# DoRA forward: W split into 125 and 3 partitions, block 0 loaded in four parts, and the last three chunks of block 4 loaded as single chunks with the first stores due one chunk earlier

## The chip, the core and the metric

The kernel runs on one core of a Trainium2 chip. The metric is the time of one execution on the device in microseconds (us). The version before the change has a median of 164.68 us over 14 runs (162.11 to 165.88).

## The reference

x has 16 x 2048 rows of 256 numbers (fp32), W is 256 x 256, lora_A 256 x 16, lora_B 16 x 256, m 256, scale 1.0.

```python
W_adapted = W + scale * (lora_A @ lora_B)
W_norm = np.sqrt(np.sum(W_adapted ** 2, axis=0, keepdims=True) + 1e-8)
W_final = W_adapted / W_norm * m
y = x.reshape(-1, 256) @ W_final
```

So 33.5 MB of x are read and 33.5 MB of y are written, and every row of x is multiplied by the same 256 x 256 matrix.

## The kernel before

**Tiling.** The 32768 rows of x are cut into 8 blocks of 4096 rows (4 MB). In a block, each of the 128 partitions holds 32 consecutive rows, 32 KB that are contiguous in device memory. A block is 8 chunks of 512 rows (4 KB per partition, 512 KB in all); the 64 chunks are numbered through, and two neighbours make a pair p (0 to 31). Block 7 is handled as two units of half a block, each contiguous per partition (16 KB). There are five block buffers `x_sb`, so blocks 5, 6 and 7 use the buffers of blocks 0, 1 and 2 again. The result of a chunk is written over its x in the same buffer, and stored from there.

**Loads** (lines 102 to 105, 139 to 142, 158 to 166). SyncE (SP) issues W first (line 150), then the list `loads` in order: chunks 0 and 1, chunks 2 to 7, then whole blocks 1 to 4. Ahead of block 5 it waits for stores 0, 1 and 2 (blocks 0, 1 and the first half of block 2; line 163), then issues block 5, block 6 and the first half of block 7; ahead of the last half block it waits for store 3. Each load has a semaphore that reaches 16 when it has landed. These DMAs run on queue q1.

**Stores** (lines 110 to 119, 144 to 147, 254 to 260). ScalarE (ACT) issues them on its queue, q10, after the small inputs lora_A, lora_B and m. Each entry of `stores` is (first chunk, chunks, chunk after which it is due). Store 0 (block 0) is due after chunk 22, store 1 after chunk 23, stores 2 and 3 (halves of block 2) after chunk 24; chunks 24 to 27 go out as four stores of 512 KB after chunk 27; the rest of block 3 and block 4 after chunk 47; the others as they are finished. Ahead of the stores of a due point, ACT waits for its own copies to drain.

**The train of one pair.** GpSimd (POOL) rounds the pair to bf16 (`xb`, line 192). TensorE (PE) transposes it as fp32 words, eight transposes (`turned`, line 297); VectorE (DVE) copies the transposed words from PSUM (`xt`, line 233); PE multiplies by `w_final`, 16 matmuls for each pair (`product`, line 311); ACT copies each chunk's result from PSUM into `x_sb` (line 251). PE's order, written out by hand, is transpose of pair p + 1, then product of pair p. POOL waits for the load that a pair is first in (line 182), for the transposes two pairs back, at pair 0 also for four steps of DVE (the square `sq`, line 187), and at pair 15 for store 2 (`REST`, line 189).

**The small work at the start.** PE transposes lora_A, multiplies by lora_B; DVE adds W (`wa`, line 214, which waits for W at line 212), squares it (line 218); PE sums the squares and spreads m over the partitions (lines 278 and 283); ACT takes the root (line 243); DVE forms `w_final` (line 229), for which PE waits at line 322.

At the end SP waits for the last ten stores in turn (line 336).

Of the kernel before, what the change touches and what calls it, by code (L numbers as in the profile page):

```python
# [11 lines left out]
def kernel(  # L12
# [10 lines left out]
    nc = tc.nc  # L23
    P = 128
# [10 lines left out]
    KC = IN // P  # L35
# [7 lines left out]
    XBUFS = 5  # L43
    CH = DJ // J
# [18 lines left out]
    def sb(name, shape, dtype):  # L63
        return ctx.enter_context(nc.sbuf_tensor(name, shape, dtype))
# [7 lines left out]
    w_nat = sb("w_nat", [P, KC, OUT], FP32)  # L72
# [28 lines left out]

    units = [(b * CH, CH) for b in range(NBLK - 1)]
    units += [(NCH - CH, CH // 2), (NCH - CH // 2, CH // 2)]
    loads = [(0, 2), (2, CH - 2)] + units[1:]
    load_of = {g: n for n, (g0, cnt) in enumerate(loads) for g in range(g0, g0 + cnt)}


# [1 line left out]

    F = NBLK - XBUFS  # L110
    G = F * CH
    stores = [(b * CH, CH, 22 + b) for b in range(F - 1)]
    stores += [(G - CH, CH // 2, 24), (G - CH // 2, CH // 2, 24)]
    FIRST = len(stores)
    stores += [(G + c, 1, G + 3) for c in range(4)]
# [9 lines left out]
    def sem(name):  # L125
        if name not in sems:
            sems[name] = tc.alloc_semaphore(name)
        return sems[name]

    def in_sbuf(g0, cnt):  # L130
        b, c = divmod(g0, CH)
        return x_bufs[b % XBUFS][:, c * J : (c + cnt) * J, :]

    def in_dram(dram, g0, cnt):
        (u0, ucnt), = [u for u in units if u[0] <= g0 < u[0] + u[1]]
        unit = dram[u0 * J * P : (u0 + ucnt) * J * P].rearrange("(p j) k -> p j k", p=P)
        return unit[:, (g0 - u0) * J : (g0 - u0 + cnt) * J, :]

    def load_x(n):
        nc.sync.dma_start(  # L140
            out=in_sbuf(*loads[n]), in_=in_dram(x_flat, *loads[n])
        ).then_inc(sem(f"load{n}"), 16)

    def store_y(n):
# [2 lines left out]
        ).then_inc(sem(f"store{n}"), 16)  # L147


    nc.sync.dma_start(  # L150
        out=w_nat[:], in_=W.rearrange("(p t) o -> p t o", t=KC)
    ).then_inc(sem("load_w"), 16)
    nc.scalar.dma_start(
        out=a_nat[:], in_=lora_A.rearrange("(p t) r -> p t r", t=KC)
    ).then_inc(sem("load_a"), 16)
    nc.scalar.dma_start(out=b_nat[:], in_=lora_B).then_inc(sem("load_b"), 16)
    nc.scalar.dma_start(out=m_row[:], in_=m[None, :]).then_inc(sem("load_m"), 16)
    for n in range(len(loads)):
        if loads[n][0] == XBUFS * CH:


            for k in range(HALF + 1):
                nc.sync.wait_ge(sem(f"store{k}"), 16)
        if loads[n] == units[-1]:
            nc.sync.wait_ge(sem(f"store{HALF + 1}"), 16)
        load_x(n)


    nc.gpsimd.memset(zeros[:], 0.0).then_inc(sem("pool"), 1)
# [2 lines left out]
        out=identity[:],  # L172
        in_=zeros[:],
# [5 lines left out]
    ).then_inc(sem("ident"), 1)  # L179
    for p in range(NPR):  # L180
        b, c = divmod(p, PRB)
        if p == 0 or load_of[2 * p - 1] != load_of[2 * p]:
            nc.gpsimd.wait_ge(sem(f"load{load_of[2 * p]}"), 16)
        if p == 0:


            nc.gpsimd.wait_ge(sem("dve"), 4)
        if p == REST:
            nc.gpsimd.wait_ge(sem(f"store{HALF}"), 16)
        if p >= NXB:  # L190
            nc.gpsimd.wait_ge(sem("turned"), p - NXB + 1)
        nc.gpsimd.tensor_copy(  # L192
            out=xb_bufs[p % NXB][:],
            in_=x_bufs[b % XBUFS][:, 2 * c * J : 2 * (c + 1) * J, :],
        ).then_inc(sem("rounded"), 1)
# [5 lines left out]
    for _ in range(IDLE):  # L201
# [7 lines left out]
    nc.vector.tensor_copy(out=b_bf[:], in_=b_nat[:])  # L209
    nc.vector.wait_ge(sem("pe"), 1)  # L210
    nc.vector.tensor_copy(out=aT[:], in_=aT_ps).then_inc(dv, 1)  # L211
    nc.vector.wait_ge(sem("load_w"), 16)
    nc.vector.wait_ge(sem("pe"), 2)
    nc.vector.scalar_tensor_tensor(  # L214
        out=wa[:], in0=ab_ps, scalar=float(scale), in1=w_nat[:], op0=ALU.mult, op1=ALU.add
# [15 lines left out]
    for p in range(NPR):  # L231
        nc.vector.wait_ge(sem("turned"), p + 1)
        nc.vector.tensor_copy(  # L233
            out=xt_bufs[p % NXT][:].rearrange("p r t -> p (r t)").bitcast(FP32),
            in_=xt_ps[p % 2][:],
# [8 lines left out]
        out=norm[:], in_=n2_ps, func=AF.Sqrt, bias=eps_col[:]  # L244
    ).then_inc(sem("act"), 1)
    drains = 0
    for g in range(NCH):
        b, c = divmod(g, CH)
# [3 lines left out]
            out=x_bufs[b % XBUFS][:, c * J : (c + 1) * J, :], in_=y_ps[g % 2][:]  # L252
# [119 lines left out]
```

## Time and profile before

| | |
|---|---|
| median of 14 runs | 164.68 us (162.11 to 165.88) |
| the profiled execution's own time | 163.09 us |
| its span, first to last instruction | 161.8 us |
| mean granted TensorE clock | 0.835 |
| busy: PE, ACT, POOL, DVE | 96.8, 64.0, 62.6, 44.9 us |
| read, written | 33.85 MB, 33.55 MB; 417 GB/s over the span |
| block load of 4 MB, issue to landing (median) | 29.1 us |
| store of 512 KB, issue to landing (median) | 47.1 us |

The profile shows one execution of the program. Its page gives busy time by engine; the span in 40 equal slices with busy tenths, the clock that TensorE was granted, the mean busy share of the 16 DMA engines and what they moved; the DMA queues (q1 is SP's, q10 ACT's); the chain of work that ended last; and groups of instructions with what ended the idle time before them. Further views are the time line, waits, DMA issues with time to landing, and windows, a table of each engine's busy time, the clock, DMA share and GB/s in chosen stretches. DMA share and bytes are counted by the slice or window in which a packet starts, so in short windows a share may exceed 1. Under these views lie the records of single DMA packets, one per partition of a transfer, and one of 4 bytes on each DMA engine when its part of a transfer is complete.

### The profile page before, as it was taken

To read this page: it belongs to the slowest core of one execution; us is meant where nothing else is said; L and a number is where in the kernel's file an instruction comes from. 1 tells how busy PE (TensorE), PEld (TensorE's weight loads), DVE (VectorE), ACT (ScalarE), POOL (GpSimd) and SP (SyncE) were. 2 spreads that over 40 slices of the span, in tenths; PEclk is the share of its full clock that TensorE was granted. 3 is DMA by queue.
4 is the path that set the end of the run, shared out by engine and by line. 5 is a ranking of instruction groups with operands and counts; after the bars stand their busy time and mean duration, and the time that the engine had idled before them with its cause. 6 is when DMAs were issued, how large, how long until landed. Compare 5 with 4: busy or idle time off the path is not lost. (4 is left out here: it accounts for less than half of the span.)

```text
span 161.8 us, 2005 instructions
## 1 busy us (share of the span) xinstructions
PE 96.8 (60%) x786; PEld 84.4 (52%) x786; DVE 44.9 (28%) x44; ACT 64.0 (40%) x67; POOL 62.6 (39%) x39
## 2 busy tenths in 40 slices
PE   0490999999999340000499969989999950000000
PEld 0250899999998220000479959979899940000000
DVE  0447335354453300000035335344444400000000
ACT  3010186777765450000036855855876760000000
POOL 1225819677672000000946269298586200000000
PEclk9999999999999955555559999999999997555555
DMA  4999999999999999999999999999999999999994
GB/s 162 462 407 468 389 510 397 389 510 397 389 510 397 389 510 397 397 444 433 413 434 420 437 440 432 385 410 416 413 446 409 486 397 429 472 397 425 425 425 199
DMA packets 3780, 67.42 MB, mean 417 GB/s; under 512 B 561, under 2 KB 578, under 8 KB 1218
## 3 DMA queue, kind: packets, MB, share of 16 engines
q1 hardware_dynamic: 1584, 33.82, 49.0%
q10 hardware_dynamic: 2194, 33.59, 48.7%
q14 instruction: 2, 0.02, 0.0%
HBM read 33.85 MB, written 33.55 MB: 417 GB/s over the span
## 5 line engine op out<-in xcount | busy, mean ns | idle before, releaser
L251 ACT COPY x_sb<-y_ps 128x1024 f32<-128x1024 f32 x64 | 62.0, 1015 | 61.1 <-PE y_ps L311 60.6
L192 POOL CAST xb<-x_sb 128x2048 bf16<-128x2048 f32 x32 | 60.1, 1893 | 62.2 <-DMA out_dram<-x_sb 27.5
L311 PE MATMUL y_ps<-w_final,xt 128*128 128x256 bf16 x512 | 64.9, 282 | 3.2 <-PEq L286 3.1
L233 DVE COPY xt<-xt_ps 128x1024 f32<-128x1024 f32 x32 | 39.2, 1225 | 75.5 <-PE xt_ps L297 75.5
L311 PEld LDWEIGHTS y_ps<-w_final,xt 128*128 128x128 bf16 x512 | 51.5, 101 | 11.2 <-issue 4.1
L297 PE MATMUL xt_ps<-identity,xb 128*128 128x128 f32 x264 | 37.2, 287 | 25.7 <-PEq L286 25.7
L297 PEld LDWEIGHTS xt_ps<-identity,xb 128*128 128x128 f32 x264 | 31.9, 149 | 28.2 <-issue 27.7
L278 PE MATMUL y_ps<-sq,ones 128*128 128x256 f32 x4 | 2.1, 674 | 1.6 <-DVE sq L218 1.6
L267 PE MATMUL y_ps<-identity,a_nat 128*16 128x128 f32 x2 | 0.6, 394 | 3.6 <-DMA a_nat<-in_lora_A_dram 3.6
L243 ACT ACTIVATE norm<-y_ps,eps_col 128x256 f32<-128x256 f32 x1 | 0.5, 473 | 5.2 <-PE y_ps L278 5.2
L278 PEld LDWEIGHTS y_ps<-sq,ones 128*128 128x128 f32 x4 | 1.2, 323 | 2.3 <-DVE sq L218 2.1
L241 ACT ACT_TABLE_LOAD x1 | 1.3, 1283 | 2.4 <-issue 2.4
L198 POOL MEMSET xb<- 128x2048 bf16 x1 | 1.8, 1804 | 0.7 <-PE xt_ps L297 0.7
L267 PEld LDWEIGHTS y_ps<-identity,a_nat 128*16 128x16 f32 x2 | 0.1, 89 | 3.6 <-issue 3.6
L226 DVE RECIPROCAL rnorm<-norm 128x256 f32<-128x256 f32 x1 | 1.7, 1745 | 0.0
L220 DVE COPY m_all<-y_ps 128x256 f32<-128x256 f32 x1 | 0.4, 425 | 3.3 <-PE y_ps L283 3.3
L283 PE MATMUL y_ps<-m_row,ones 1*128 1x256 f32 x2 | 1.2, 710 | 0.0
L209 DVE CAST b_bf<-b_nat 16x256 bf16<-16x256 f32 x1 | 0.3, 281 | 2.9 <-DMA b_nat<-in_lora_B_dram 2.9
L271 PE MATMUL y_ps<-b_bf,aT 16*128 16x256 bf16 x2 | 0.6, 402 | 0.6 <-DVE aT L211 0.6
L214 DVE SCALAR_TENSOR_TENSOR wa<-y_ps,w_nat 128x512 f32<-128x512 f32 x1 | 0.7, 692 | 0.8 <-PE y_ps L271 0.8
L283 PEld LDWEIGHTS y_ps<-m_row,ones 1*128 1x128 f32 x2 | 0.5, 308 | 0.7 <-issue 0.7
L229 DVE TENSOR_TENSOR w_final<-wam,rnorm 128x256 bf16<-128x256 f32 x2 | 0.8, 422 | 0.0
(13 smaller groups left out, 3.3 us busy)
## 6 DMA issues: line engine op xcount, KB each, us to landing
x_sb<-in_x_dram SPq DMA_DIRECT2D x6, 4096.0 KB, 29.1
out_dram<-x_sb ACTq DMA_DIRECT2D x5, 4096.0 KB, 21.0
out_dram<-x_sb ACTq DMA_DIRECT2D x5, 2048.0 KB, 28.9
x_sb<-in_x_dram SPq DMA_DIRECT2D x2, 2048.0 KB, 34.0
x_sb<-in_x_dram SPq DMA_DIRECT2D x1, 3072.0 KB, 12.0
out_dram<-x_sb ACTq DMA_DIRECT2D x4, 512.0 KB, 47.1
x_sb<-in_x_dram SPq DMA_DIRECT2D x1, 1024.0 KB, 5.1
w_nat<-in_W_dram SPq DMA_DIRECT2D x1, 256.0 KB, 2.9
```

The lines of the kernel that those rows point to most:

```text
L192: nc.gpsimd.tensor_copy(out=xb_bufs[p % NXB][:], in_=x_bufs[b % XBUFS][:, 2 * c * J : 2 * (c + 1) * J, :],).then_inc(sem("rounded"), 1)
L198: nc.gpsimd.memset(xb_bufs[NPR % NXB][:], 0.0).then_inc(sem("rounded"), 1)
L214: nc.vector.scalar_tensor_tensor(out=wa[:], in0=ab_ps, scalar=float(scale), in1=w_nat[:], op0=ALU.mult, op1=ALU.add).then_inc(dv, 1)
L226: nc.vector.reciprocal(out=rnorm[:], in_=norm[:]).then_inc(dv, 1)
L229: i = nc.vector.tensor_mul(out=w_final[:, t], in0=wam[:, t], in1=rnorm[:])
L233: nc.vector.tensor_copy(out=xt_bufs[p % NXT][:].rearrange("p r t -> p (r t)").bitcast(FP32), in_=xt_ps[p % 2][:],).then_inc(sem("copied"), 1)
L241: nc.scalar.activation(out=warm[:], in_=eps_col[:], func=AF.Sqrt)
L251: nc.scalar.copy(out=x_bufs[b % XBUFS][:, c * J : (c + 1) * J, :], in_=y_ps[g % 2][:]).then_inc(sem("room"), 1)
L278: i = nc.tensor.matmul(n2_ps, ones[:], sq[:, t, :], start=(t == 0), stop=(t == KC - 1))
L283: nc.tensor.matmul(mb_ps, ones[0:1, :], m_row[:], start=True, stop=True).then_inc(pe, 1)
L297: i = nc.tensor.transpose(xt_ps[p % 2][:, j * P : (j + 1) * P], xb_bufs[p % NXB][:, j, :].bitcast(FP32), identity[:],)
L311: i = nc.tensor.matmul(y_ps[h][:, j, :], xt_bufs[p % NXT][:, r : r + P, t], w_final[:, t, :], start=(t == 0 and (j % (J // 2)) == 0), stop ...
```

## The change

1. Block 0 is loaded in four parts rather than two: chunk 0, chunk 1, chunks 2 and 3, chunks 4 to 7.
2. W goes in two transfers: partitions 0 to 124 on SP's queue after the load of chunk 0, and partitions 125 to 127 on ACT's queue between lora_B and m. DVE waits for 32 on W's semaphore instead of 16.
3. Block 4 is loaded as its first five chunks (20 KB per partition) and then its last three as single chunks (4 KB per partition), all ahead of SP's wait for stores 0 to 2.
4. Stores 0 and 1 are due after chunks 21 and 22 instead of 22 and 23.
5. POOL waits for the loads of both chunks of a pair, since these can be different ones.

The order on PE, DVE and POOL and the number of their instructions stay the same; SP issues five more DMAs and ACT one more.

```diff
-    loads = [(0, 2), (2, CH - 2)] + units[1:]
+    loads = [(0, 1), (1, 1), (2, 2), (4, CH - 4)] + units[1 : XBUFS - 1]
+    loads += [((XBUFS - 1) * CH, CH - 3)]
+    loads += [(XBUFS * CH - 3 + c, 1) for c in range(3)] + units[XBUFS:]
...
-    stores = [(b * CH, CH, 22 + b) for b in range(F - 1)]
+    stores = [(b * CH, CH, 21 + b) for b in range(F - 1)]
...
-    nc.sync.dma_start(
-        out=w_nat[:], in_=W.rearrange("(p t) o -> p t o", t=KC)
-    ).then_inc(sem("load_w"), 16)
+    W_CUT = 125
+    def load_w(engine, p0, p1):
+        engine.dma_start(
+            out=w_nat[p0:p1], in_=W.rearrange("(p t) o -> p t o", t=KC)[p0:p1]
+        ).then_inc(sem("load_w"), 16)
     nc.scalar.dma_start(
         out=a_nat[:], in_=lora_A.rearrange("(p t) r -> p t r", t=KC)
     ).then_inc(sem("load_a"), 16)
     nc.scalar.dma_start(out=b_nat[:], in_=lora_B).then_inc(sem("load_b"), 16)
+    load_w(nc.scalar, W_CUT, P)
     nc.scalar.dma_start(out=m_row[:], in_=m[None, :]).then_inc(sem("load_m"), 16)
...
         load_x(n)
+        if n == 0:
+            load_w(nc.sync, 0, W_CUT)
...
-        if p == 0 or load_of[2 * p - 1] != load_of[2 * p]:
-            nc.gpsimd.wait_ge(sem(f"load{load_of[2 * p]}"), 16)
+        for g in (2 * p, 2 * p + 1):
+            if g == 0 or load_of[g - 1] != load_of[g]:
+                nc.gpsimd.wait_ge(sem(f"load{load_of[g]}"), 16)
...
-    nc.vector.wait_ge(sem("load_w"), 16)
+    nc.vector.wait_ge(sem("load_w"), 32)
```

## The prediction, made before the changed kernel was run

> **What bounds the kernel now.** I read the page first: chain, busy slices and DMA queues. Then the end of the run in windows of a microsecond, the start in windows, and the handover from loads to stores in ScalarE's time line.
>
> ```profile
> PE 10%; ACT 1%; ACTq 1%; issue 0%
> ...
> DMA  4999999999999999999999999999999999999994
> GB/s 162 462 407 468 389 510 397 389 510 397 389 510 397 389 510 397 397 444 433 413 434 420 437 440 432 385 410 416 413 446 409 486 397 429 472 397 425 425 425 199
> DMA packets 3780, 67.42 MB, mean 417 GB/s; under 512 B 561, under 2 KB 578, under 8 KB 1218
> ...
> q1 hardware_dynamic: 1584, 33.82, 49.0%
> q10 hardware_dynamic: 2194, 33.59, 48.7%
> ```
>
> The chain covers only a tenth of the span: computing stops near 133 us and the last 29 us are stores. All 16 DMA engines are busy in every slice but the first and the last (49.0 + 48.7 = 97.7% of the span). So the time is start + each DMA engine's own work + its idle time, and it ends with the engine that is last. PE, ACT and POOL are far from it.
>
> ```profile
> 158.00:159.00 1.00, 0.00 (x0) 0.00 (x0) 0.00 (x0) 0.00 (x0) 0.00 (x0) 0.50 1.11 475
> 159.00:160.00 1.00, 0.00 (x0) 0.00 (x0) 0.00 (x0) 0.00 (x0) 0.00 (x0) 0.50 0.39 164
> 160.00:161.00 1.00, 0.00 (x0) 0.00 (x0) 0.00 (x0) 0.00 (x0) 0.00 (x0) 0.50 0.12 49
> 161.00:161.80 0.80, 0.00 (x0) 0.00 (x0) 0.00 (x0) 0.00 (x0) 0.00 (x0) 0.50 0.00 0
> ```
>
> The last two columns are DMA share and GB/s. After 159 only 0.51 engine-microseconds per engine are left, yet the span runs to 161.8: the engines don't end together. The 16 completion packets of the last store give the ends: eleven at 159.3 to 159.7, then 160.2, 160.3, 160.55, 161.2 and 161.4. (The trace keeps each packet's size, start and duration, not its engine; durations below are these.) The two last engines cost 1.7 us against the eleven.
>
> ```profile
> 0.00:2.00 2.00, 0.00 (x0) 0.00 (x0) 0.17 (x2) 0.00 (x0) 0.70 (x6) 1.00 0.02 5
> 2.00:3.00 1.00, 0.00 (x0) 0.00 (x0) 0.00 (x0) 0.62 (x1) 0.00 (x0) 1.00 0.46 161
> 3.00:4.00 1.00, 0.35 (x2) 0.12 (x2) 0.00 (x0) 0.86 (x2) 0.00 (x0) 1.00 1.13 451
> ```
>
> In the third microsecond, under W, the engines are half empty; from 3 us on they are full.
>
> ```profile
> 45.94 1.93 ACT L251 COPY x_sb<-y_ps 128x1024 f32<-128x1024 f32 x2 [0.69 <-PE y_ps L311]
> 48.56 1.01 ACT L251 COPY x_sb<-y_ps 128x1024 f32<-128x1024 f32 x1 [0.69 <-PE y_ps L311]
> 49.68 0.37 ACTq L145 DMA_DIRECT2D out_dram<-x_sb  x1
> ```
>
> Chunks 20 and 21 are drained at 47.87, chunk 22 at 49.57, and the first store issues. Block 4's loads end at 51.80 to 52.2 (their completion packets), and on each engine the first store packet follows at once: no gap here.
>
> **The change, part by part**, on the engines' own work.
>
> *W.* 128 rows now run as 8 packets of 84 ns on each engine, 0.67 us. How 125 rows are shared no row shows. Every transfer in the trace gives its engines equal shares: 16 completions for 128 and for 16 rows, one for m's single row. Bounds: all 16 engines, nothing added; one engine, 125 x 84 ns = 10.5 us, so +9.8. Equal shares on more than one engine leave only 5 engines of 25 rows (125 = 5x5x5). I take that: +25x84 - 8x84 = +1.43 us on five, -0.67 on eleven. The 3 rows add at most 3 x 84 ns, 0.25 on one engine; I take one row, 0.08.
>
> [...]
>
> *Smaller descriptors.* Block 0 per engine: 8x309 + 8x912 ns become 16x159 + 8x309 + 8x611, +0.14 us. Block 4: 8x1213 become 8x762 (20 KB, between 611 and 912) + 24x159, +0.21. Five more completions of 9 ns: 0.04. Sum +0.39. Bounds: 4 KB packets take 159 ns between 32 KB ones, but about two dozen of them, 4 KB stores that ran alone at 81 to 83 us, took 305. Alone run chunks 0 and 1 (16 packets) and the 15 or so before stores join, so 31 x 0.146 = up to +4.5. Below nothing: none, a smaller packet is never faster per byte in these rows. I take 159, since the nearest rows by direction, reads alone, keep pace: 309 ns for 8 KB with the same 32 KB pitch, 84 for 2 KB.
>
> [...]
>
> *Start.* W's 0.67 us of work took 1.2 to 1.5 us (first packet 1.98, completions 3.19 to 3.49): packets arrived slower than they moved. Chunk 0's packets are twice as long, 1.27 us, at the same count, so the engines fill. Gain between 0 and 0.7; I take -0.5 on all.
>
> *W later, and the wait for 32.* On DVE, sq, m_all and w_final queue behind it; POOL's first cast and PE's norm wait for sq. W lands near 1.98 + 1.27 + 2.1 = 5.4 on the five; DVE reached it at 5.53, after PE. Worth 0 to +0.5 there. Chunks 2 and 3 land near 9 instead of 13.4 with the rest of the block, so the first product comes some 3 us earlier than 17.64. But block 1 lands on the five 1.15 us behind its former time (1.43 + 0.08 + 0.14 - 0.5), about 0.7 after the one engine that set it. POOL rounded it at 23.59 to 25.48 and PE took it at 25.62, so PE waits and its train is 0.7 later than before. Chunk 21 is done at 48.6 rather than 47.87.
>
> *First stores.* Issued at 48.7 instead of 49.68. a_nat's first packet came 1.0 us after its issue, so store packets can run from 49.7; the eleven engines have loads until 51.80 - 0.8 = 51.0. The margin was 51.8 - 50.7 = 1.1 and becomes 1.3. Nothing gained in this profile, where there was no gap. The extra issue on ACT and the five on SP (0.4 to 0.5 us each) come long before their data's turn; m lands 0.4 later, under a use at 9.01. The last chunks alternate with 24 store packets and land near 77; POOL, whose waits now name them, wants chunk 37 at 85.50: hidden by 8 us.
>
> *Reload.* Store 2 lands up to 1.0 us later on the five, so SP's loads of block 5 come at about 78 instead of 77.14. Queued are store 3 and the four 512 KB stores, 4.2 MB or 9.7 us, against 4.3 us from issue to the first packet at 81.5: costs nothing, unless it grows by 5 us. The last store is issued at 132.8 and lands at 161.4, so 28 us of queue hide any delay of the computing: nothing.
>
> Sum: five engines +1.43 + 0.39 - 0.5 = +1.3; eleven -0.67 + 0.39 - 0.5 = -0.8. Case A: neither of the two last engines (161.2, 161.4) is among the five. These fall to 160.6; the end is the latest of the five, 159.7 + 1.3 = 161.0, or 161.5 to 161.85 if one of the 160.2 to 160.55 is among them (77% if drawn blindly). Against 161.4: -0.4 to +0.5, taken +0.3. Case B: one of the two is: 162.5 to 162.7, +1.3. Drawn blindly A has 46%. m's single row, followed by packets that start as another ends, leads to an engine that ends early; if it is one of the five, A has 52%.
>
> The profiled execution took 163.09 us (span 161.8 and 1.3 around it), the median is 164.68. A gives 163.4 there and 165.0 against the median; B 166.0.
>
> **Rivals.** (1) Slower: 4 KB loads alone run at 305 ns as the stores did. For it: the rows at 81 to 83. Against: reads at 2 and 8 KB. Price +2.3 at the start alone, +4.5 with the handover: 167.3 to 169.5. It decides from about 210 ns per packet (31 x 51 ns = 1.6 us). (2) Faster: the median's extra 1.6 us over the profiled run is a gap at the handover, which a margin of 1.1 us makes possible; stores a chunk earlier close it, and the five are engines that end early: 164.68 - 1.6 - 0.4 = 162.7. Against: the margin grows by 0.2 only. (3) W on one engine: +9.8, 174; or on all 16: -0.1, 164.6. (4) The last chunks don't run beside stores, because chunk 21 is later than the loads' end: nothing gained or lost, 165.
>
> **How the numbers follow.** A 0.36 (with 4 and W on 16), B 0.30, rival 1 0.18, rival 2 0.14, one engine 0.02. A is likeliest: 165.0; its own range 164.3 to 165.2. The range from rival 2's price to the low part of rival 1: 162.7 to 167.6 leaves out some 2 in 10. About 1%, 1.65 us, is what a measurement of this kernel tells from no change: below 163.0 lies most of rival 2, 0.13; above 166.3 rival 1, one engine and B's tail, 0.22; the rest 0.65.
>
> **What would show it.** W's 84 ns packets on five engines, 25 each; chunk 0's packets of 159 or 305 ns; DMA share in the third microsecond near 0.9; the first store issue at 48.7; the reload at 78; in the last windows, which engines end late. I am wrong if 4 KB reads alone are slow, if the late engines are settled by something that the change moves, or if the median held a gap that the profile lacks.

## The result, and the profile after the change

The changed kernel takes 166.12 us in the median (10 runs, 165.81 to 166.66), the kernel before 164.45 us (47 runs, 162.11 to 165.88): 1.016 times, 95% interval 1.013 to 1.0189. It is slower by 1.6%; the two medians alone are 1.0% apart. The time lies in the predicted range (162.7 to 167.6), 1.1 us above the predicted 165.0. It is also just inside the band of 163.0 to 166.3 that the prediction thought likeliest, but that band stood for no clear change, and the change is clear. Ratios here and below are taken over the fast runs of both kernels (those up to 1.5% above the fastest of the same kernel), so they are not exactly the ratios of the medians.

The profiled execution took 166.3 us with a span of 165.0, 3.2 us more than the profiled one of before. From its page:

```profile
DMA  4999999999999999999999999999999999999993
GB/s 110 273 397 479 433 437 413 421 461 429 402 425 407 476 410 422 461 411 417 421 419 381 453 424 428 458 385 429 413 448 489 389 445 437 407 477 393 421 413 131
DMA packets 4492, 67.42 MB, mean 409 GB/s; under 512 B 633, under 2 KB 650, under 8 KB 1930
...
q1 hardware_dynamic: 2290, 33.81, 49.4%
q10 hardware_dynamic: 2200, 33.60, 47.8%
```

The DMA engines are as busy as before, 97.2% of a longer span, and the bytes are the same. So a busy DMA engine must have moved less in its time. The row of GB/s says where: 110 and 273 in the first two slices, where it was 162 and 462. Windows of the start (the last three columns are granted clock, DMA share and GB/s):

```profile
2.00:3.00 1.00, 0.00 (x0) 0.00 (x0) 0.00 (x0) 0.31 (x1) 0.00 (x0) 1.00 0.57 113
3.00:4.00 1.00, 0.00 (x0) 0.00 (x0) 0.00 (x0) 0.99 (x2) 0.00 (x0) 1.00 0.76 279
4.00:10.00 6.00, 1.19 (x4) 0.25 (x4) 0.82 (x3) 0.19 (x1) 0.00 (x0) 1.00 1.02 297
```

The same six microseconds of the kernel before:

```profile
4.00:10.00 6.00, 3.83 (x10) 1.79 (x8) 2.00 (x4) 0.47 (x1) 1.89 (x1) 1.00 1.05 448
```

The share is 1.02 and 1.05, full in both; 297 against 448 GB/s is the difference. In the packet records, between 6 and 8 us, 8 KB packets took 492 ns on average (309 is their usual time), 4 KB ones 229 (159) and W's 2 KB ones 142 (84). W has 125 packets with five completions on q1, and three with three completions on q10: it went to five engines and to three.

The whole train moved back with the start. POOL's time line after:

```profile
11.37 3.91 POOL L205 CAST xb<-x_sb 128x2048 bf16<-128x2048 f32 x2 [9.70 <-DVE sq L231]
18.28 1.89 POOL L205 CAST xb<-x_sb 128x2048 bf16<-128x2048 f32 x1 [2.99 <-DMA x_sb<-in_x_dram]
...
27.99 5.57 POOL L205 CAST xb<-x_sb 128x2048 bf16<-128x2048 f32 x3 [5.08 <-DMA x_sb<-in_x_dram]
```

The first cast waits for `sq`, which waits for W, until 11.37; the last of these lines is block 1, at 27.99. In the kernel before it was at 23.59:

```profile
23.59 5.57 POOL L192 CAST xb<-x_sb 128x2048 bf16<-128x2048 f32 x3 [3.77 <-DMA x_sb<-in_x_dram]
```

ACT's time line at the handover:

```profile
50.34 1.93 ACT L264 COPY x_sb<-y_ps 128x1024 f32<-128x1024 f32 x2 [0.69 <-PE y_ps L324]
52.38 0.38 ACTq L149 DMA_DIRECT2D out_dram<-x_sb  x1
```

The first store is issued at 52.38, after chunk 21, where it was 49.68 after chunk 22. And the end, in windows:

```profile
160.00:161.00 1.00, 0.00 (x0) 0.00 (x0) 0.00 (x0) 0.00 (x0) 0.00 (x0) 0.50 0.99 426
161.00:162.00 1.00, 0.00 (x0) 0.00 (x0) 0.00 (x0) 0.00 (x0) 0.00 (x0) 0.50 0.46 197
162.00:163.00 1.00, 0.00 (x0) 0.00 (x0) 0.00 (x0) 0.00 (x0) 0.00 (x0) 0.50 0.34 147
163.00:164.00 1.00, 0.00 (x0) 0.00 (x0) 0.00 (x0) 0.00 (x0) 0.00 (x0) 0.50 0.15 66
```

All 16 engines work to 161; then about a third of them goes on (0.34 of 16 is five) until 164.5. The completions of the last store say the same: eleven at 161.45 to 161.76, five at 163.34, 163.60, 163.65, 163.93 and 164.54. Two things have been added: all engines end 2 us later than the eleven early ones of before (159.3 to 159.7), and five end another 1.6 to 3.1 us behind these.

### The profile page after: what moved, and what is told of

Read it like the earlier page. It is cut to its first block, busy times and chain, and to the rows that moved or that the text cites. A ratio compares the mean times of both kernels' runs of the same rounds, so it can differ in the third digit from the quotient of the medians.

```text
span 165.0 us, 2014 instructions
## 1 busy us (share of the span) xinstructions
PE 96.8 (59%) x786; PEld 84.5 (51%) x786; DVE 45.0 (27%) x44; ACT 64.0 (39%) x67; POOL 62.6 (38%) x39
## 5 line engine op out<-in xcount | busy, mean ns | idle before, releaser
L236 DVE TENSOR_TENSOR wam<-wa,m_all 128x256 f32<-128x256 f32 x2 | 0.9, 496 | 0.0
```

What stands on the lines that cost most here:

```text
L236: i = nc.vector.tensor_mul(out=wam[:, t], in0=wa[:, t], in1=m_all[:])
```

## Experiments

Theories. **I**: W's rows on five engines make these late (the prediction's step). **W**, called **C** where it is tried away from the start: while five engines move such rows, the others move their own data more slowly. **P**: the small parts of block 0 are slow by themselves (the prediction's rival 1, at the start). **G**: stores that are issued earlier save time at the handover. S and D are set out with the runs that try them. In the diffs three dots stand for lines that only follow from the ones shown (waits, the allocation of a tile).

### Block 0 in four parts, alone

```diff
-    loads = [(0, 2), (2, CH - 2)] + units[1:]
+    loads = [(0, 1), (1, 1), (2, 2), (4, CH - 4)] + units[1:]
...
```

> The kernel before with one part of the change: block 0 loaded in four parts (chunks 0; 1; 2 and 3; 4 to 7), W still first and in one transfer of 128 partitions. In the changed kernel the DMA engines moved only about 295 GB/s from 4 to 10 us, where the kernel before moved 420 to 430. Theory P (small parts): the 4 KB and 8 KB descriptors of block 0 at a pitch of 32 KB are slow; then the slow stretch is here too, all engines lose about 2 us, block 1 lands about 2 us later than 23.35 and the time is 1.0 to 1.3% above the kernel before. Theory W (W's 125 rows on five engines beside the other engines' loads make all slow): no slow stretch here, block 1 lands within 0.4 us of before, the time is within 0.3% of before.

Measured: 162.98 us, 0.9897 of the kernel before (0.9854 to 0.994). The parts don't slow the kernel; against the kernel before of this series it is 1% faster. In the profile 4 KB packets took 159 to 168 ns between 3 and 6 us; a few 8 KB packets behind them were slow (up to 998 ns between 6 and 7 us), and 0.8 us for each engine went into slow packets before 12 us, against 2.2 in the changed kernel. P falls. Why this kernel gains 1% its profile doesn't show: that execution, at 163.66 the slowest of its six, issued its first store at 50.79.

### W in 125 and 3 rows, alone

```diff
-    nc.sync.dma_start(
-        out=w_nat[:], in_=W.rearrange("(p t) o -> p t o", t=KC)
-    ).then_inc(sem("load_w"), 16)
...
+    load_w(nc.scalar, W_CUT, P)
...
         load_x(n)
+        if n == 0:
+            load_w(nc.sync, 0, W_CUT)
...
```

> The kernel before with one part of the change: W in transfers of 125 and 3 partitions, the 125 behind the first load (chunks 0 and 1, 8 KB descriptors) on SP's queue, the 3 on ACT's queue. Theory I (imbalance alone): five engines get 25 rows of W and end about 2 us behind the other eleven (1.43 us more work, the others 0.67 less); the slow stretch is absent; time +0.6 to +0.9% over before. Theory W (five engines' reading of W slows all): the same spread at the end and in addition 295 GB/s between 4 and 8 us; time +1.5 to +2%. Theory P (small parts alone are slow): as under I.

Measured: 167.97 us, 1.0208 of the kernel before (1.0162 to 1.0254), more than the whole change. Both I and W are seen. W's rows moved from 5.1 to 8.6 us. Between 6 and 8 us the other eleven engines' 24 KB packets took 1365 to 1374 ns on average, and 920 again after 9 us (912 is usual). The five engines ended block 4's loads at 54.56 to 54.91, the eleven at 52.37 to 52.73. And here the late train opened a gap, since this kernel lacks the other half of the change. Its windows at the handover:

```profile
50.00:52.00 2.00, 2.00 (x21) 1.89 (x19) 0.83 (x1) 1.34 (x2) 1.34 (x2) 1.00 1.03 442
52.00:54.00 2.00, 2.00 (x21) 1.89 (x19) 0.61 (x2) 1.93 (x2) 1.27 (x2) 1.00 0.38 164
54.00:56.00 2.00, 2.00 (x21) 1.87 (x20) 1.01 (x1) 1.01 (x1) 1.71 (x1) 1.00 0.00 0
56.00:58.00 2.00, 1.89 (x18) 1.49 (x17) 1.22 (x1) 1.28 (x2) 0.00 (x0) 1.00 1.20 508
```

PE is busy throughout while no DMA engine starts anything from 54 to 56: the loads are done, the first store is issued at 55.78, its first packet runs at 56.65. The eleven idle for 4.0 us, the five for 1.9. The changed kernel's windows at the same place show no such hole:

```profile
50.00:52.00 2.00, 2.00 (x20) 1.88 (x19) 0.70 (x1) 1.66 (x2) 1.40 (x1) 1.00 0.95 389
52.00:54.00 2.00, 2.00 (x21) 1.83 (x19) 1.22 (x1) 1.28 (x2) 1.88 (x1) 1.00 1.09 438
54.00:56.00 2.00, 1.89 (x19) 1.52 (x17) 1.23 (x1) 1.43 (x2) 0.01 (x1) 1.00 1.28 543
```

### The changed kernel with W whole

```diff
-    W_CUT = 125
+    W_CUT = P
...
-    load_w(nc.scalar, W_CUT, P)
...
-    nc.vector.wait_ge(sem("load_w"), 32)
+    nc.vector.wait_ge(sem("load_w"), 16)
```

> The changed kernel with W in one transfer of 128 partitions, in the same place behind chunk 0's load. Theory I: the five late engines vanish, all 16 complete their last store within about 1 us; the time falls by 1.2 us or more against the changed kernel, to 164.9 or below, and to about 163 if the slow start goes with it (theory W). Theory P: the start stays at about 295 GB/s from 4 to 10 us, so block 1 still lands near 27 us, and the time stays near 165. If neither I nor W holds, the time stays at 166.1.

Measured: 162.72 us, 0.9893 of the kernel before (0.9853 to 0.9934), so 3.4 us under the changed kernel. Its windows:

```profile
4.00:10.00 6.00, 2.88 (x8) 1.42 (x8) 2.08 (x4) 0.00 (x0) 1.59 (x1) 1.00 1.06 433
...
159.00:160.00 1.00, 0.00 (x0) 0.00 (x0) 0.00 (x0) 0.00 (x0) 0.00 (x0) 0.50 0.35 148
160.00:161.00 1.00, 0.00 (x0) 0.00 (x0) 0.00 (x0) 0.00 (x0) 0.00 (x0) 0.50 0.08 33
161.00:162.00 1.00, 0.00 (x0) 0.00 (x0) 0.00 (x0) 0.00 (x0) 0.00 (x0) 0.50 0.04 16
```

433 GB/s instead of 297 in the start, and no group of five at the end: thirteen engines end at 159.37 to 159.79, three later (160.18, 161.01, 161.79). The cut of W at 125 is the whole loss. The rest of the change gains about 1% against the kernel before of this series; the later series show less.

### The handover alone

```diff
-    loads = [(0, 2), (2, CH - 2)] + units[1:]
+    loads = [(0, 2), (2, CH - 2)] + units[1 : XBUFS - 1]
+    loads += [((XBUFS - 1) * CH, CH - 3)]
+    loads += [(XBUFS * CH - 3 + c, 1) for c in range(3)] + units[XBUFS:]
...
-    stores = [(b * CH, CH, 22 + b) for b in range(F - 1)]
+    stores = [(b * CH, CH, 21 + b) for b in range(F - 1)]
...
```

> The kernel before with the other part of the change alone: block 4's last three chunks as single loads, and stores 0 and 1 due a chunk earlier; W and block 0 as before. Theory of the prediction: 24 smaller packets cost 0.2 us, the handover had no gap, so the time is within 0.3% of the kernel before. Rival: the median execution of the kernel before holds a gap at the handover that its profile lacks (164.45 against the profiled 163.09); then this one is 0.5 to 1% faster, and its spread over runs smaller.

Measured: 162.84 us, 0.9953 (0.9909 to 0.9998), nine runs between 162.57 and 163.74. Half a per cent faster, with an interval that nearly reaches 1, and a narrower spread: the rival's side rather than the prediction's.

### The kernel before, once more

No edit.

> The kernel before, unchanged, for a second profile of it. Its runs spread from 162.1 to 165.9 while those with the last chunks of block 4 loaded alone and stores a chunk earlier spread from 162.6 to 163.7. Theory G (gap): where this execution takes 164.3 or more, its profile shows a gap at the handover near 52 us, DMA share and GB/s clearly under those of the first profile, with the first store's issue later than 49.68. Rival: the extra lies in the ends of the engines (a later last engine) or in the stretches at 80 to 83 and 113 to 116 us, with no gap at 52. If it takes about 163 again, this run tells nothing of it.

Measured: 163.48 us. The first store was issued at 50.12, and thirteen of its first packets took 1430 ns on average instead of 1213: 0.2 us for each engine, and no idle engine. At 163.48 this execution is near the median of its series (163.38), so it says nothing of those at 165.

### W cut at 112

(against the changed kernel)

```diff
-    W_CUT = 125
+    W_CUT = 112
```

> The changed kernel with W cut at 112 instead of 125: as many transfers in the same places, but 112 and 16 rows, which all 16 engines share equally (7 and 1 each). Theory I (few engines: W's five engines are late, and their reading slows the others): no slow start, no group of five late at the end, time within 0.3% of W in one transfer behind chunk 0 (162.7), so 162.3 to 163.3. Rival (a split W as such, its second transfer on ACT's queue or the wait for 32, costs): the time stays near 166.1, or half way if it is a part.

Measured: 162.96 us, 0.9962 of the kernel before in this series (0.9929 to 0.9995), ten runs between 162.72 and 163.13. W in two transfers, on two queues, with the wait for 32, costs nothing to speak of when the rows are 112 and 16, which share out evenly over 16 engines. Windows:

```profile
4.00:10.00 6.00, 3.13 (x8) 1.41 (x8) 2.00 (x4) 0.33 (x2) 1.84 (x2) 1.00 1.06 399
...
159.00:160.00 1.00, 0.00 (x0) 0.00 (x0) 0.00 (x0) 0.00 (x0) 0.00 (x0) 0.50 0.54 229
160.00:161.00 1.00, 0.00 (x0) 0.00 (x0) 0.00 (x0) 0.00 (x0) 0.00 (x0) 0.50 0.08 33
```

All engines end between 159.48 and 160.89. The start is between the two others, 399 GB/s.

### The same 125 rows later, beside 32 KB loads

This is the changed kernel with W whole; it reads 125 of W's rows a second time into a tile that nothing uses.

```diff
...
+        if n == 4:
+            nc.sync.dma_start(
+                out=spare[0:125], in_=W.rearrange("(p t) o -> p t o", t=KC)[0:125]
+            ).then_inc(sem("load_d"), 16)
```

> The changed kernel with W in one transfer of 128 rows, and in addition the same 125 rows of W read once more into a spare tile, behind block 1's load, that is beside 32 KB loads at about 23 us (extra work, for no use in the result). Theory C (company: rows read by five engines slow whatever the other eleven load): for some 3 us the 32 KB packets of the eleven take 1.4 to 1.5 times 1213 ns; all engines lose about 1 us, the five end 2 us or more behind; time 165.5 to 166.5. Theory S (slow only at the start of the program): 32 KB packets stay at 1213 to 1222; the five end 2.1 us behind and the time is 164.3 to 165.0.

Measured: 165.84 us, 1.015 of the kernel before (1.0101 to 1.02). Its windows:

```profile
18.00:22.00 4.00, 4.00 (x27) 3.46 (x26) 1.23 (x1) 1.06 (x2) 1.89 (x1) 1.00 1.12 483
22.00:26.00 4.00, 4.00 (x39) 3.71 (x38) 1.92 (x2) 2.79 (x3) 1.38 (x1) 1.00 1.03 306
26.00:30.00 4.00, 4.00 (x39) 3.74 (x37) 1.76 (x2) 3.12 (x4) 4.00 (x3) 1.00 0.95 397
...
160.00:161.00 1.00, 0.00 (x0) 0.00 (x0) 0.00 (x0) 0.00 (x0) 0.00 (x0) 0.50 0.54 229
161.00:162.00 1.00, 0.00 (x0) 0.00 (x0) 0.00 (x0) 0.00 (x0) 0.00 (x0) 0.50 0.31 131
162.00:163.00 1.00, 0.00 (x0) 0.00 (x0) 0.00 (x0) 0.00 (x0) 0.00 (x0) 0.50 0.19 82
```

From 22 to 26 us 306 GB/s at a share of 1.03, where the changed kernel with W whole, and without the extra rows, has 426:

```profile
22.00:26.00 4.00, 4.00 (x35) 3.74 (x33) 1.23 (x1) 2.40 (x3) 1.89 (x1) 1.00 0.99 426
```

The eleven's 32 KB packets took 1923 ns on average between 24 and 25 us, 1.59 times 1213, and 1219 again after 27; the rows themselves took up to 147 ns instead of 84. At the end eleven engines complete at 160.49 to 160.96 and five at 162.56 to 164.03. C holds and S falls: it isn't the start, and it isn't small x loads; it is the 125 rows.

### W whole and first

```diff
+    load_w(nc.sync, 0, W_CUT)
     for n in range(len(loads)):
...
-        if n == 0:
-            load_w(nc.sync, 0, W_CUT)
```

(against the changed kernel with W whole)

> The changed kernel with W in one transfer of 128 rows and first on SP's queue, as in the kernel before: all of the change but W's split and place. W behind chunk 0 gave 162.72. If W first empties the third microsecond (prediction's start gain of 0.5 us) this one is about 0.5 us slower, 163.2; if the order doesn't matter, 162.7; 4 KB parts behind W had a slow stretch from 6 to 10 us (386 GB/s) when tried alone, which would make it 163.5.

Measured: 162.76 us, 0.9985 of the kernel before in this series (0.9947 to 1.0023), against 162.72 for W behind chunk 0. The order makes no difference that these medians show. The kernel before has a median of its own in each series of runs (164.61, 163.38 and 164.35 us, each on another chip), while the versions of the changed kernel with W shared by 16 engines stay at 162.7 to 163.0. So how much the rest of the change gains isn't settled: about 1% in the first series, 0.2 to 0.4% in this one.

### The 125 rows without SBUF, and without device memory

Two kernels with the extra transfer of above, once from device memory to device memory, once within SBUF; each ran once. The edits are against the kernel with the extra rows.

```diff
-    spare = sb("spare", [P, KC, OUT], FP32)
+    spare = nc.dram_tensor("spare_dram", [P, KC, OUT], FP32, kind="Internal").ap()
```

> The run with the extra 125 rows behind block 1's load, but the rows now go from device memory to a spare place in device memory instead of to SBUF (extra work, for no use in the result). There the 32 KB packets of the eleven other engines rose from 1213 to as much as 1946 ns. Theory D (device memory: five engines that read and write neighbouring rows hold up the others' reads): the 32 KB packets rise here too, to 1.4 times or more. [...]

Measured: 163.38 us, and 32 KB packets at 1213 to 1215 from 18 to 29 us. This doesn't decide: the records show the transfer as 16 packets of 16000 bytes, 596 ns each, and not as 125 rows of 2 KB, so it was never a transfer of such rows on five engines.

```diff
+            nc.sync.wait_ge(sem("load_w"), 16)
             nc.sync.dma_start(
-                out=spare[0:125], in_=W.rearrange("(p t) o -> p t o", t=KC)[0:125]
+                out=spare[0:125], in_=w_nat[0:125]
```

> As before, but the extra 125 rows are copied within SBUF, from W's tile to a spare tile (SP waits until W has landed ahead of it; extra work, for no use in the result). Theory D (device memory): the 32 KB packets of the others stay within 3% of 1213. [...]

Measured: 166.47 us. One window:

```profile
22.00:26.00 4.00, 4.00 (x36) 3.70 (x35) 1.23 (x1) 2.64 (x4) 1.35 (x1) 1.00 0.95 298
```

298 GB/s, and 32 KB packets at 1922 ns on average between 25 and 26 us while the rows moved (23.9 to 26.7). But 32 KB packets of 1421 to 1648 ns on average, up to 2136, came already from 20 to 23.9 us, ahead of the first 2 KB packet in the records, and cost as much: 0.8 us for each engine against 0.7 beside the rows. That stays unexplained, so neither the window nor the time of this kernel is the rows' doing alone. It speaks against D, in one execution: the extra transfer read no row from device memory, and while its rows moved the others were held up as much.

### Stores earlier alone, and the last chunks alone

```diff
-    stores = [(b * CH, CH, 22 + b) for b in range(F - 1)]
+    stores = [(b * CH, CH, 21 + b) for b in range(F - 1)]
```

> The kernel before with stores 0 and 1 due one chunk earlier, and nothing else. Both halves of the handover together gave 0.9953 of the kernel before, and the gap after block 4's loads grew with the time of the first store's issue (none at 49.68, small at 50.12, about 0.7 us at 50.79, about 3.5 us at 55.78). Theory G (the earlier issue closes the gap): first store near 48.0, no gap at 52, time 0.3 to 0.8% under the kernel before. Rival (the single chunks do it): no difference, within 0.2%.

Measured: 163.24 us, 0.9938 of the kernel before (0.9908 to 0.9968). The first store is issued at 48.01. The gain is as large as that of both parts of the handover together, so the earlier stores are enough for it. But it is not a gap closed, as far as the profile goes: the last 32 KB loads, which began at 50.58 to 50.82 us, ahead of the first store packet at 52.45, took 1964 ns on average, 0.75 us more for each engine, and the execution was still one of the fastest (162.43).

```diff
-    loads = [(0, 2), (2, CH - 2)] + units[1:]
+    loads = [(0, 2), (2, CH - 2)] + units[1 : XBUFS - 1]
+    loads += [((XBUFS - 1) * CH, CH - 3)]
+    loads += [(XBUFS * CH - 3 + c, 1) for c in range(3)] + units[XBUFS:]
...
```

> The kernel before with block 4's last three chunks as single loads, stores due as before. Theory G: the first store comes near 49.7 to 50.1 and the loads end at 52 as before, so nothing is gained and 24 smaller packets cost 0.2 us: within 0.3% of before. Rival (the single chunks do it): 0.3 to 0.8% faster, with 4 KB packets landing well beyond 53 us between 32 KB store packets.

Measured: no verdict. Two of the six runs took 162.6 us and four 165.1 to 165.6. The 4 KB loads ran alone from 48 to 51 us at 160 to 163 ns on average.

## Why the prediction was right or wrong

**The number and the sum.** The time lies in the range, but the sum behind 165.0 lacks its largest term: it forecast +0.3 us, and the change cost 1.7. The range held the time by luck, since it reached up to 167.6 for rival 1, which the runs refute. That case B's 166.0 comes near 166.12 is luck as well. Of the mechanism, W on five engines was right, and what this does to the other eleven was missing.

**W on five engines: right, and too small.** The five completions show the sharing that the step took. Its two groups were to end 2.1 us apart; the spread at the end is 1.6 to 3.1 us. The size was too small because the step priced W's packets at 84 ns, as they ran when all engines read W; beside other work they took 123 on average, so 25 of them took 3.1 us. Sixteen completions for 112 rows, and sixteen for 16, came with W cut at 112.

**What W does to the others: missing.** No step of the prediction had it. It priced each engine's own work as if the engines didn't meet. Slow packets before 12 us cost each engine 2.2 us in the changed kernel and 0.7 with W whole; the eleven, which the sum had 0.8 us earlier, end 2 us later (161.6 against 159.5). With the extra rows beside 32 KB loads the loss was as large: the 32 KB packets between 21 and 28 us took 1.5 us longer than usual for each of eleven engines. This term, some 1.5 us on all engines, and the larger lag turned +0.3 (case A) into +1.7.

**The start, -0.5 us: wrong.** The DMA share in the third microsecond was 0.57, not near 0.9. With W whole, where the start can be seen by itself, W first gives 162.76 and W behind chunk 0 gives 162.72, so filling the third microsecond's empty engines gained nothing that shows. With W behind it, chunk 0's packets that began before 3 us took 376 ns on average in place of 159, so it seems that x lost the time instead that W's slow arrival had lost.

**Small descriptors, 159 ns for 4 KB reads alone: right.** Rival 1, 305 ns, is refuted twice: 159 to 168 ns at 3 to 6 us in the kernel with four parts, 160 to 164 at 48 to 54 us in several. One profile differs: with W whole and first, 4 KB loads took 241 ns on average at 50 to 51 us, up to 574, ahead of the first store packet at 51.98, though that execution took only 162.79. No run measured the +0.39 by itself. So the 305 ns of the stores at 81 to 83 us are not a property of 4 KB packets as such.

**The train, 0.7 us later: wrong by a lot.** Chunk 21 was done at 52.27, not 48.6. The prediction let W land at 5.4; the slow start held it until DVE could begin at 9.79, and block 1 until 27.99. lora_A's small packets came late as well: PE began at 6.73, not 3.65.

**The reload: later, but right that it costs nothing.** POOL's wait for store 2 ended at 81.47, 4.4 us later than before and not 1.0, and the first packet of block 5 came at 85.06. The engines still had stores to move: the DMA share is 0.92 or more in the windows of 2 us from 80 to 86.

**First stores, "nothing gained": half right.** In the changed kernel the handover took a train that was 4.4 us late without a hole; the split of W without it opened one of 4.0 us on eleven engines. So this part saved the changed kernel from a further loss, which the higher time of W's split alone (167.97 against 166.12) agrees with. Alone it gains 0.5%, from the earlier stores. Rival 2 had that gain as a gap in the median execution; neither profile of the kernel before has one, and no execution near 165 us was profiled. Where those lose their time stays open.

**Which engines end late: case B by size, neither by cause.** The engines that ended late in the first profile (160.2 to 161.4) were taken as fixed. In the changed kernel the eleven end within 0.3 us of each other; in its own windows at 114 to 118 us (412 and 438 GB/s) there is little left of the slow stretch (348 and 332 GB/s from 113 to 115 in the kernel before). The second profile of the kernel before has another pattern, six engines at 160.6 to 161.7. So the lateness belongs to the execution, and chances counted over one profile had no base.

## What to carry to other kernels

Where all 16 DMA engines are busy from start to end, choose a row count that shares out evenly over them, as 128 and 112 did here (162.72 and 162.96 us): 125 rows instead of 128 put a quarter megabyte on five engines and cost 3.4 us of 163. Price such a transfer twice, on its own engines (123 ns for each 2 KB row instead of 84) and on the others, whose packets took 1.5 to 1.6 times their usual time beside it. Read GB/s beside the DMA share: here a share of 1.02 went with 297 GB/s and one of 1.05 with 448. The difference was slow packets, which no idle time showed.

## What the runs showed that I had not expected

While five engines moved rows of 2 KB to 125 consecutive partitions, the other eleven's packets took 1.5 to 1.6 times their usual time (24 KB: 912 to 1374 ns; 32 KB: 1213 to 1923), at the start and at 24 us, whether the rows came from device memory or, in one execution, from SBUF, and the total fell from about 430 to between 297 and 350 GB/s. Such packets are not proof of a transfer on few engines, though: they came without one too, at 20 to 22 us in the copy within SBUF (up to 2136 ns) and at 50 us with the stores earlier alone (1964 on average); what slowed those stays open. Rows of 112, seven for each of 16 engines, did this only slightly (399 GB/s against 433 in the six microseconds). Why the others slow down is not shown: the copy within SBUF, which read no row from device memory, did the same harm while its rows moved, but in that run as much was lost ahead of them; the transfer meant to leave SBUF out ran as 16 packets of 16000 bytes; and the records name neither the engine nor the partition of a packet.

The price of a 4 KB packet also depended on its company: 305 ns for 22 stores at 81.0 to 82.5 us, where the first loads of block 5 came in, 159 for stores beside 32 KB loads after that, 162 for loads alone. And the first packets of x are slow when they open the program: up to 3 us 8 KB ones took 710 ns on average (W's split alone), 4 KB ones 376 (the changed kernel with W whole). W's 2 KB ones in the same place took 85 in the kernel before, and 91 to 130 in six other profiles that opened with W.
